# The border between mixer and up projection in a set order per engine, with the second pair's raw weights and a second h tile in finished rows

## The chip, the cores and the metric

The kernel runs on one core of a Trainium2 chip. The metric is the device time of one execution in microseconds (us); the figure of a kernel is the median of three runs. TensorE is called PE here, its weight loads PEld, VectorE DVE, ScalarE ACT, GpSimd POOL, and SyncE, which issues all the DMAs, SP.

## The reference

One layer of a streaming encoder for 1024 prompt frames and 64 sample frames, model width 1024. It has a mixer (two kinds of attention and a gating block, then one output projection) and an MLP with squared ReLU, each followed by a residual sum and a layer norm. What counts here is the seam between the two:

```python
x = layer_norm(ALPHA * x + mix, ln1_g, ln1_b)            # (1024 + 64, 1024)
h = jnp.square(jax.nn.relu(x @ w_up))                    # w_up   (1024, 4096)
x = layer_norm(ALPHA * x + h @ w_down, ln2_g, ln2_b)     # w_down (4096, 1024)
```

## The kernel before

Matrices are multiplied in three fp32r passes (high x high, high x low, low x high): every operand is split into a rounded copy, which ACT writes, and the rest, which DVE or POOL subtracts (`split`, `lo_sub`, L97).

**The mixer's tail.** Frames stand in nine tiles of 128 rows (the ninth has the 64 sample rows), taken in the order 0, 1, 4, 5, 8, 2, 6, 3, 7. `mix(t)` multiplies a tile with w_out (L232), adds the residual (L237) and norms it (`layer_norm`, L125 to L139): moments on DVE, the inverse root on POOL, scaling on ACT, the gain on POOL, the bias on DVE. The result, x1, stays in a tile `y` (tag `row`, seven buffers) and is stored to DRAM (L249).

**The up projection** is a Strassen-like scheme. Per pair p of weight blocks (256 of the 4096 columns, two f halves of 128) seven products stand in for eight. Seven combinations of the frames (`xo`) are made once by `x_pair`: transposes of y tiles on PE (L1127), sums (L1142 to L1151), splits. The frames are in two sets: s=0 (288 columns: tiles 0, 1, 4, 5 and the samples) and s=1 (256: tiles 2, 3, 6, 7). Seven combinations of W_up are made per pair by `prep`: three are splits of the raw weights (`wa`, L1182, the rest on POOL), four come from `w_sums` (L1190 to L1193, DVE, in place over the raw weights) and are split after that (`ws`, L1457 and L97).

A `Chain(p, s)` does the seven products of pair p and set s, twelve matmuls each (L1242). PSUM banks: A three times in turn, B, C, and D twice. ACT copies the A banks (L1253); DVE adds the banks into h (L1256 to L1262). The seventh product opens bank D again, so it must wait until L1256 has read D. Then come `relu` (L1274) and `sums` (L1283 to L1286) and the stores of h to DRAM (L1287, L1288, L1291).

**The border** is pair 0 and the start of pair 1. Pair 0's raw weights are loaded early; chain (0, 0) and then chain (0, 1) keep h in one set of buffers, `h7` (tag `wq`, one buffer) and `h1`. All mixer tiles lie in a pool `sp`. Only when it is closed (`p12.close()`) is the pool `lp` opened, over the same addresses, and pair 1's raw weights `wr1` are loaded into it. Pairs 1 to 12 run both chains product by product.

**What sets the order.** A scheduler places each engine's instructions by its own estimates, except inside `in_order(...)`, which chains every instruction of an engine to the one recorded before it. In the kernel before that is used only at the later border, from the up to the down projection.

Of the kernel before, what the change touches and what calls it, by code (L numbers as in the profile page):

```python
# [56 lines left out]
def _build(nc, tc, a, es):  # L57
# [151 lines left out]
    def mix(t, sa):  # L209
# [7 lines left out]
        y = ys[t] = two_halves(f"y{t}", None, None)  # L217
# [3 lines left out]
        for half in range(2):  # L221
# [46 lines left out]
    with ExitStack() as p1:  # L268
        sa = p1.enter_context(tc.tile_pool(name="sa", bufs=1, side="right"))

# [481 lines left out]
        def sgu_v(wv):  # L752
            wst = sp.tile([P, 4, 2, P], F32R, name="wst", tag="cc0")
# [5 lines left out]
            bs = sp.tile([P, 4], F32, name="bs")  # L759
# [351 lines left out]
    xs = p12.enter_context(tc.tile_pool(name="xs", bufs=1, side="right", reuse_waits="tile"))  # L1111
# [7 lines left out]
    def x_steps(nm, s, c0, n, r0, n0, r1, n1):  # L1119
# [31 lines left out]
        nc.vector.tensor_tensor(tt[:, 3], tt[:, 1], p21, op=ALU.subtract)  # L1151
        if s == 0:
# [160 lines left out]
    x23 = [x_pair(2), x_pair(3)]  # L1313
# [4 lines left out]
    def x_next(n):  # L1318
        for _ in range(n):
            while x23:  # L1320
                if next(x23[0], StopIteration) is StopIteration:
                    x23.pop(0)
                    continue
                break

    def first_chain(s, weave):
# [5 lines left out]
        h7 = sp.tile([P, 7, NS[s]], F32, name=f"h7_{s}", tag="wq", bufs=1)  # L1332
        h1 = sp.tile([P, 1, NS[s]], F32, name=f"h1_{s}", tag="raw", bufs=2)

        def hh(a, b):

            if a == 4:
                return h1
            return h7[:, a:b] if b <= 4 else h7[:, a - 1:b - 1]

        ch = Chain(0, s, Some(), hh, ((2, 4), (4, 5), (5, 6)))
        for i in range(7):
            ch.product(i)
            if weave:
                x_next(2)

    x_next(3)
    first_chain(0, True)
    x_next(99)
    first_chain(1, False)  # L1350
    p12.close()


    lp = es.enter_context(tc.tile_pool(name="lp", bufs=1, side="left", reuse_waits="tile"))
# [84 lines left out]
    with ExitStack() as p3:  # L1439
        rp = p3.enter_context(rp)  # L1440

        def prep(p, rest=True):
            raw = lp.tile([P, KT, 256], F32, name=f"wr{p}", tag="wr")
            nc.sync.dma_start(raw, w_up[:, :, p * 256:(p + 1) * 256])
# [3 lines left out]
            f0, f1 = raw[:, :, 0:P], raw[:, :, P:256]  # L1448
            a, b = slice(0, 4), slice(4, 8)
            for o, src in ((0, f0[:, a]), (1, f0[:, b]), (2, f1[:, b])):  # L1450
                split(wa[:, o, 0], wa[:, o, 1], src, nc.gpsimd)
            def summed():
                w_sums(f0, f1)

            def high():
                for q in (a, b):
                    nc.scalar.activation(ws[:, 0, q], raw[:, q], AF.Copy)  # L1457

            def low():
                lo_sub(nc.vector, ws[:, 1], raw, ws[:, 0])  # L1460
# [14 lines left out]
        prep(1)  # L1475
        for p in range(1, NP - 3):
# [524 lines left out]
```

## Time and profile before

| what | value |
|---|---|
| median of 3 runs | 1420.37 us (1419.03 to 1420.98) |
| profiled execution | 1420.73 us, span 1419.0 us |
| PE busy in the span | 1327.6 us (94%), 8827 matmuls |
| DVE / ACT / POOL busy | 1000.0 (70%) / 720.6 (51%) / 612.2 (43%) us |
| chain that ended last, by engine | PE 62%, DVE 11%, DMA 8%, POOL 7% |

The span runs from the first to the last instruction; what is left of the execution's time, 1.7 us, lies around it. In the timeline views a row is a run of like instructions in time: start, time from the start of its first to the end of its last, engine, line and tiles, count, and in square brackets the idle time of the engine just before it with what ended it.

### The profile page before, as it was taken

The numbers are of one execution on the slowest core, as the hardware profiler recorded it, in microseconds if no ns is written. First come the engines' busy times: TensorE is split into PE (matmuls) and PEld (weight loads), VectorE is DVE, ScalarE is ACT, GpSimd is POOL, SyncE is SP. The second block draws the span as 40 slices with busy tenths as digits, with TensorE's granted clock in tenths as the row PEclk, the third lists the DMA queues.
The fourth block names the chain that finished last, engine by engine and source line by source line (L and its number), as shares of the span: only waits on it lengthen the run. The fifth ranks groups of instructions, "written<-read, shape, count | busy, mean of one in ns | idle before, by whom it ended". The sixth has DMA issues, their size and how long they took to land.

```text
span 1419.0 us, 24283 instructions
## 1 busy us (share of the span) xinstructions
PE 1327.6 (94%) x8827; PEld 1210.9 (85%) x8827; DVE 1000.0 (70%) x1797; ACT 720.6 (51%) x1561; POOL 612.2 (43%) x665
## 2 busy tenths in 40 slices
PE   7999999999989997998969999999989999999996
PEld 6899999999888996876859999999977778887875
DVE  3567566676786599877836787687668677677676
ACT  3366555666664475333413332322237677667765
POOL 2222222266564446655412222122146765555647
PEclk9999999999999998999989999999999999999999
DMA  7324232322313424432033443443378343344343
GB/s 216 77 78 112 61 109 66 81 66 55 79 27 83 130 86 135 130 108 78 32 112 116 166 138 116 165 138 124 134 233 300 118 165 136 122 160 140 109 134 127
DMA packets 148177, 168.86 MB, mean 119 GB/s; under 512 B 27085, under 2 KB 114445, under 8 KB 148057
## 3 DMA queue, kind: packets, MB, share of 16 engines
q1 hardware_dynamic: 148056, 167.30, 37.8%
q8 instruction: 70, 1.15, 0.3%
q14 instruction: 51, 0.41, 0.1%
HBM read 109.26 MB, written 51.71 MB: 113 GB/s over the span
## 4 chain that ended last, share of the span: by engine, by line
PE 62%; DVE 11%; DMA 8%; POOL 7%; issue 5%; ACT 5%; SPq 1%; DVEq 0%; ACTq 0%; POOLq 0%
PE zA L1242 9%; PE zD L1242 6%; PE mx L232 6%; PE kvsb L337 5%; PE kvfox L337 4%; PE A L1630 4%; PE zB L1242 3%; PE zC L1242 3%; DMA rd<-w_down 2%; POOL rd L1387 2%; POOL wd L97 2%; PE qfox L478 2%; PE qsb L478 2%; PE Sfox L536 2%; PE D L1630 2%
## 5 line engine op out<-in xcount | busy, mean ns | idle before, releaser
L97 POOL TENSOR_TENSOR wa<-wr,wa 128x512 fp32r<-128x512 f32 x45 | 67.9, 1536 | 232.0 <-ACT wa L1182 232.0
L97 POOL TENSOR_TENSOR wd<-rd,wd 128x512 fp32r<-128x512 f32 x77 | 101.5, 1328 | 123.4 <-ACT wd L1182 113.5
L232 PE MATMUL mx<-xT,oTb 128*128 128x512 f32 (+1 forms) x416 | 107.0, 409 | 3.3 <-ACT oTb L191 2.3
L1242 PE MATMUL zD<-xo,ws 128*128 128x288 f32 (+1 forms) x720 | 99.1, 292 | 8.6 <-DVE hh L1256 8.6
L1242 PEld LDWEIGHTS zD<-xo,ws 128*128 128x128 f32 x720 | 94.9, 191 | 9.3 <-DVE hh L1256 9.3
L232 PEld LDWEIGHTS mx<-xT,oTb 128*128 128x128 f32 (+1 forms) x416 | 77.5, 191 | 23.1 <-ACT oTb L191 3.3
L1242 PE MATMUL zA<-xo,ws 128*128 128x288 f32 (+1 forms) x720 | 97.1, 289 | 0.0
L337 PE MATMUL kvfox<-wkvfox,xT 128*128 128x256 f32 (+3 forms) x624 | 91.3, 296 | 3.0 <-DVE fx L440 1.9
L1242 PEld LDWEIGHTS zA<-xo,ws 128*128 128x128 f32 x720 | 93.5, 189 | 0.0
L522 POOL TENSOR_TENSOR sgsb<-sgsb,snsb 128x127 f32<-128x127 f32 (+7 forms) x48 | 58.8, 1227 | 78.4 <-DVE snsb L520 63.9
L1182 ACT ACTIVATE wd<-rd 128x512 fp32r<-128x512 f32 x105 | 63.9, 624 | 55.3 <-POOL rd L1387 26.4
L337 PE MATMUL kvsb<-wkvsb,xT 128*128 128x256 f32 (+1 forms) x624 | 87.7, 286 | 0.0
L1387 POOL TENSOR_TENSOR rd<-rd 128x512 f32<-128x512 f32 x56 | 79.7, 1423 | 17.7 <-DVE b L97 15.4
L337 PEld LDWEIGHTS kvfox<-wkvfox,xT 128*128 128x128 f32 (+1 forms) x624 | 82.5, 196 | 4.6 <-DVE fx L440 2.2
L1630 PE MATMUL A<-wd,wd 128*128 128x512 f32 x312 | 82.5, 396 | 3.0 <-DVE acc L1597 2.8
L520 DVE TENSOR_TENSOR_SCAN snsb<-snsb,one 128x128 f32<-128x128 f32 (+7 forms) x48 | 72.1, 1506 | 13.2 <-ACT snsb L519 12.7
L1253 ACT ACTIVATE sn<-zA 128x256 f32<-128x256 f32 (+1 forms) x80 | 31.1, 390 | 95.8 <-PE zA L1242 86.4
L337 PEld LDWEIGHTS kvsb<-wkvsb,xT 128*128 128x128 f32 (+1 forms) x624 | 79.2, 187 | 0.2
L1630 PEld LDWEIGHTS A<-wd,wd 128*128 128x128 f32 x312 | 58.2, 188 | 18.6 <-DVE acc L1597 4.1
L1630 PE MATMUL A<-wd,h4a 128*128 128x512 f32 x240 | 64.6, 394 | 0.0
L1242 PE MATMUL zA<-xo,wa 128*128 128x288 f32 (+1 forms) x360 | 50.2, 293 | 10.2 <-ACT wa L1182 10.2
L1457 ACT ACTIVATE ws<-wr 128x1024 fp32r<-128x1024 f32 x30 | 31.1, 1057 | 56.0 <-DVE wr L1192 56.0
(524 smaller groups left out, 3748.7 us busy)
## 6 DMA issues: line engine op xcount, KB each, us to landing
wr<-w_up SPq DMA_DIRECT2D x15, 1024.0 KB, 5.5
h_dr<-hh SPq DMA_DIRECT2D x30, 512.0 KB, 3.2
rd<-w_down SPq DMA_DIRECT2D x30, 512.0 KB, 4.3
awa<-h_dr SPq DMA_DIRECT2D x30, 512.0 KB, 4.0
hr<-h_dr SPq DMA_DIRECT2D x32, 384.0 KB, 4.7
h_dr<-hh SPq DMA_DIRECT2D x30, 384.0 KB, 4.2
raw<-w_in SPq DMA_DIRECT2D x44, 256.0 KB, 3.4
xr<-x_prompt SPq DMA_DIRECT2D x8, 512.0 KB, 6.5
```

Source lines behind the costliest of these rows:

```text
L97: eng.tensor_tensor(out, src, hi.bitcast(F32), op=ALU.subtract)
L232: nc.tensor.matmul(acc[0:m], oT[:, k, hx, 0:m], wo[k // 4][hw][:, k % 4, cs], start=(i == 0), stop=(i == len(seq) - 1))
L337: nc.tensor.matmul(acc[0:n, c0:c0 + n1 - n0], xT[k // 4][:, k % 4, c:c + n], wt[:, k, hw, n0:n1], start=(i == 0), stop=(i == len(seq) - 1))
L478: nc.tensor.matmul(acc[:, 0:w], wq[:, k, hw, :], xT[k // 4][:, k % 4, c:c + w], start=(i == 0), stop=(i == len(seq) - 1))
L520: nc.vector.tensor_tensor_scan(g[:, 0:n][:, ::-1], g[:, 0:n][:, ::-1], one.broadcast_to([P, n]), 1.0, op0=ALU.mult, op1=ALU.bypass)
L522: nc.gpsimd.tensor_tensor(s[:, 0:n - 1], s[:, 0:n - 1], g[:, 1:n], op=ALU.mult)
L1182: nc.scalar.activation(hi, raw, AF.Copy)
L1242: nc.tensor.matmul(z, w[:, hw, k], xop(s, bo, hx)[:, k, :], start=(new and k == 0 and j == 0), stop=(k == 3 and j == 2), skip_group_check= ...
L1253: nc.scalar.activation(c, z, AF.Copy)
L1387: eng.tensor_tensor(r[:, o], r[:, x], r[:, y], op=ALU.subtract)
L1457: nc.scalar.activation(ws[:, 0, q], raw[:, q], AF.Copy)
L1630: nc.tensor.matmul(z, h[:, hx, q, o], wset[self.c % 2][q][:, hw, wb], start=((n in (0, 3) or n == 1 and self.c == 0) and q == 0 and j == 0 ...
```

## The change

It does the following.

- `layer_norm` becomes a generator `norm_steps` in three steps (moments, scale and gain, bias); for the last mixer tile, 7, the steps are taken one by one in the border.
- The border, from tile 7's norm to pair 1's first chain, is recorded inside `in_order(border)`.
- Pair 1's raw W_up is loaded as two f halves of 512 KB into the rows of x1 of tiles 2 and 6 (`raws1`), whose values have been stored and transposed. `prep` takes such a pair of halves; its splits and sums then work on two tiles of 128x8x128, not on one of 128x8x256.
- Chain (0, 1) keeps h in the rows of tiles 3 and 7 (`h44`), not in the tile of chain (0, 0).
- `lp` is opened ahead of chain (1, 0), which is recorded whole inside the set order; then come `prep(2)` and chain (1, 1), which the scheduler places. Pairs from 2 on are recorded as before.
- Three small tiles (`sel2`, `wst`, `bs`) move from pool `sp` to `sa`, and the pool `xs` of the transposes gets an exit of its own.

```diff
-            nc.vector.tensor_tensor(h, h, bb[0:n, c], op=ALU.add)
+            if not acts:
+                nc.vector.tensor_tensor(h, h, bb[0:n, c], op=ALU.add)
+        yield
...
+        h44 = [yrow[t].rearrange("p (b c) -> p b c", b=4) for t in (3, 7)]
+        return Chain(0, s, Some(), lambda a, b: h44[a // 4][:, a % 4:(b - 1) % 4 + 1], ((2, 4), (4, 6)))
...
-    x_next(3)
-    first_chain(0, True)
-    x_next(99)
-    first_chain(1, False)
-    p12.close()
...
+    with in_order(border):
+        ln = norm_steps(sp, ys[t], P, env["g1"], env["b1"], f"a{t}", True)
+        next(ln)
+        next(x2)
+        c0 = first_chain(0)
+        c0.product(0)
...
+        raws1 = [yrow[t].rearrange("p (k c) -> p k c", k=KT) for t in (2, 6)]
+        for f in range(2):
+            nc.sync.dma_start(raws1[f], w_up[:, :, 256 + f * P:256 + (f + 1) * P])
+        x1_store(t)
...
+        c1 = first_chain(1)
+        c1.product(0)
+        for _ in x3:
+            pass
+        c1.product(1)
+        c0.relu()
+        c1.product(2)
+        c0.sums()
+    xss.close()
...
+        with in_order(border):
+            summed, high, low = prep(1, False, raws1)
+            c1.product(3)
+            summed()
+            c1.product(4)
+            high()
+            c1.product(5)
+            low()
+            c1.product(6)
+        p12.close()
+
+        lp = es.enter_context(tc.tile_pool(name="lp", bufs=1, side="left", reuse_waits="tile"))
+        with in_order(border):
+            ch = chain(1, 0)
+            for i in range(7):
+                ch.product(i)
+        prep(2)
```

The built programs differ in the border alone: on PE the 2054 rows of the program ahead of it and the 827 rows from pair 4's second product on are the same. In the rows below, names have lost the first number: `zA_0_` is bank A of set 0, `zA_1_` of set 1; `y_8335`, `y_8482`, `y_8592` and `y_8676` are the rows of x1 of tiles 2, 6, 3 and 7. The lines of the changed kernel are 20 higher in the Chain (L1256 becomes L1276, L1274 becomes L1294, L1283 to L1286 become L1303 to L1306), L1190 to L1193 become L1210 to L1213.

PE, the end of pair 0 and the start of pair 1, before:

```order
L1242 MATMUL zC_1_9035<-xo_8760,w_3_8716 128x256 x2
L1242 MATMUL zA_1_8967<-xo_8760,oTb 128x256 x12
L1242 MATMUL zC_1_9035<-xo_8760,w_3_8716 128x256 x10
L1242 MATMUL zD_1_9008<-xo_8759,oTb 128x256 x12
L1242 MATMUL zA_0_9117<-xo_7973,wa_9081 128x288
L1242 MATMUL zA_1_9131<-xo_8759,wa_9081 128x256
L1242 MATMUL zB_0_9145<-xo_7973,wa_9081 128x288
L1242 MATMUL zB_1_9159<-xo_8759,wa_9081 128x256
```

and in the changed kernel:

```order
L1262 MATMUL zD_1_9020<-xo_8744,oTb 128x256 x12
L1262 MATMUL zA_1_8947<-xo_8745,oTb 128x256 x12
L1262 MATMUL zC_1_9053<-xo_8745,w_3_8716 128x256 x12
L1262 MATMUL zD_1_9020<-xo_8744,oTb 128x256 x12
L1262 MATMUL zA_0_9096<-xo_7973,wa_9012 128x288 x12
L1262 MATMUL zB_0_9110<-xo_7973,wa_9012 128x288 x12
L1262 MATMUL zA_1_9218<-xo_8744,wa_9012 128x256 x12
L1262 MATMUL zB_1_9232<-xo_8744,wa_9012 128x256 x12
```

Products are whole there; the last one of pair 0 (bank D for the second time) still stands just ahead of pair 1.

DVE, the end of chain (0, 0) and the start of chain (0, 1), before:

```order
L1274 SCALAR_TENSOR_TENSOR h_0_8796<-h_0_8796 128x576
L1283 TENSOR_TENSOR h_0_8796<-h_0_8797,h_0_8796 128x256
L1286 TENSOR_TENSOR h_0_8796<-h_0_8796,h_0_8797 128x256
L1284 TENSOR_TENSOR h_0_8796<-h_0_8796 128x256
L1285 TENSOR_TENSOR h_0_8796<-h_0_8796 128x256
L1258 TENSOR_TENSOR h_1_8965<-zB_1_8981,sn_1_0_8962 128x256
L1256 TENSOR_TENSOR h_1_8965<-zD_1_9008,sn_1_2_8964 128x256
```

and in the changed kernel:

```order
L1278 TENSOR_TENSOR y_8592<-zB_1_8969,sn_1_0_8944 128x256
L1294 SCALAR_TENSOR_TENSOR h_0_8829<-h_0_8829 128x576
L1294 SCALAR_TENSOR_TENSOR h_0_8830<-h_0_8830 128x288
L1294 SCALAR_TENSOR_TENSOR h_0_8829<-h_0_8829 128x288
L1303 TENSOR_TENSOR h_0_8829<-h_0_8830,h_0_8829 128x256
L1304 TENSOR_TENSOR h_0_8829<-h_0_8829 128x256
L1305 TENSOR_TENSOR h_0_8829<-h_0_8829 128x256
L1306 TENSOR_TENSOR h_0_8829<-h_0_8829,h_0_8830 128x256
L1210 TENSOR_TENSOR y_8482<-y_8482 128x512
L1211 TENSOR_TENSOR y_8482<-y_8335,y_8482 128x512
L1212 TENSOR_TENSOR y_8335<-y_8482,y_8335 128x512
L1213 TENSOR_TENSOR y_8335<-y_8335 128x512
L1276 TENSOR_TENSOR y_8676<-zD_1_9020,sn_1_2_8946 128x256
```

The first add of chain (0, 1) has moved ahead of chain (0, 0)'s end, and the four sums of pair 1's weights stand ahead of the add that frees bank D.

SP, the stores and loads of the border, before:

```order
L249 DMA x_dr<-y_8592 128x512 x2
L249 DMA x_dr<-y_8676 128x512 x2
L1291 DMA hs_dr<-h_0_8796 128x32
L1291 DMA hs_dr<-h_0_8797 128x32
L1291 DMA hs_dr<-h_0_8796 128x2x32
L1287 DMA h_dr<-h_0_8796 512x1x256
L1288 DMA h_dr<-h_0_8796 384x1x256
L1287 DMA h_dr<-h_1_8965 128x1024
L1288 DMA h_dr<-h_1_8965 128x768
L1444 DMA wr_9079<-w_up 128x8x256
L1444 DMA wr_9096<-w_up 128x8x256
```

and in the changed kernel:

```order
L267 DMA x_dr<-y_8592 128x512 x2
L1381 DMA y_8335<-w_up 128x8x128
L1381 DMA y_8482<-w_up 128x8x128
L267 DMA x_dr<-y_8676 128x512 x2
L1307 DMA h_dr<-h_0_8829 512x1x256
L1308 DMA h_dr<-h_0_8829 384x1x256
L1311 DMA hs_dr<-h_0_8829 128x2x32
L1311 DMA hs_dr<-h_0_8830 128x32
L1311 DMA hs_dr<-h_0_8829 128x32
L1307 DMA h_dr<-y_8592 128x1024
L1308 DMA h_dr<-y_8676 128x768
L1491 DMA wr_9199<-w_up 128x8x256
```

Pair 1's weights have moved from behind both chains' stores to ahead of tile 7's store; pair 2's load is now the first behind them.

## Rows read from the trace of the kernel before

**Rows 1.** Busy time per stretch: bounds, length, PE, PEld, DVE, ACT, POOL; PEclk, DMA, GB/s.

```profile
700.00:720.00 20.00, 15.45 (x116) 14.96 (x116) 14.22 (x25) 5.48 (x11) 4.07 (x3) 0.91 0.19 63
720.00:730.00 10.00, 0.04 (x1) 0.04 (x1) 2.12 (x6) 0.72 (x2) 0.00 (x0) 0.65 0.59 197
730.00:740.00 10.00, 10.00 (x67) 9.96 (x68) 5.12 (x6) 3.76 (x6) 3.75 (x3) 0.83 0.01 2
...
800.00:1000.00 200.00, 200.00 (x1589) 200.00 (x1588) 151.90 (x220) 55.72 (x105) 48.00 (x30) 1.00 0.42 141
```

**Rows 2.** Timeline of PE through the border, from the mixer's last products to pair 2.

```profile
676.01 11.37 PE L232 MATMUL mx<-xT,oTb 128*128 128x512 f32 x48
687.22 0.60 PE L1127 MATMUL xta<-ident,y 128*128 128x128 f32 x4
687.65 0.60 PE L1127 MATMUL xtd<-ident,y 128*128 128x128 f32 x4
...
696.51 1.86 PE L1242 MATMUL zA<-xo,oTb 128*128 128x288 f32 x12 [1.72 <-ACT sn L1253]
...
700.44 0.66 PE L1127 MATMUL xtd<-ident,y 128*128 128x128 f32 x4 [0.88 <-DVE h L1256]
...
702.52 1.57 PE L1242 MATMUL zA<-xo,w 128*128 128x256 f32 x12
...
716.78 2.93 PE L1242 MATMUL zD<-xo,oTb 128*128 128x256 f32 x12 [3.83 <-DVE h L1256]
729.96 0.82 PE L1242 MATMUL zA<-xo,wa 128*128 128x288 f32 x2 [10.24 <-ACT wa L1182]
...
731.62 3.68 PE L1242 MATMUL zA<-xo,wa 128*128 128x288 f32 x22
...
741.19 2.96 PE L1242 MATMUL zA<-xo,ws 128*128 128x288 f32 x22
...
759.17 1.77 PE L1242 MATMUL zC<-xo,wa 128*128 128x288 f32 x12
760.78 3.07 PE L1242 MATMUL zA<-xo,ws 128*128 128x288 f32 x23
```

**Rows 3.** Timeline of DVE in the same stretch.

```profile
695.85 1.75 DVE L139 TENSOR_TENSOR y<-y,gb 128x512 f32<-128x512 f32 x1 [2.29 <-POOL y L138]
...
704.40 1.28 DVE L97 TENSOR_TENSOR xo<-tt,xo 128x512 fp32r<-128x512 f32 x2
...
708.73 0.76 DVE L1274 SCALAR_TENSOR_TENSOR h<-h 128x576 f32<-128x576 f32 x1
709.41 1.52 DVE L1283 TENSOR_TENSOR h<-h,h 128x256 f32<-128x256 f32 x1
...
715.98 0.42 DVE L1258 TENSOR_TENSOR h<-zB,sn 128x256 f32<-128x256 f32 x1 [3.92 <-DMA h_dr<-h]
...
733.83 0.69 DVE L1190 TENSOR_TENSOR wr<-wr 128x512 f32<-128x512 f32 x1 [11.60 <-POOL wa L97]
...
736.00 0.69 DVE L1193 TENSOR_TENSOR wr<-wr 128x512 f32<-128x512 f32 x1
```

**Rows 4.** Timeline of POOL in the same stretch.

```profile
709.08 1.57 POOL L97 TENSOR_TENSOR xo<-tt,xo 128x512 fp32r<-128x512 f32 x1 [2.26 <-ACT xo L1160]
730.04 3.75 POOL L97 TENSOR_TENSOR wa<-wr,wa 128x512 fp32r<-128x512 f32 x3 [19.39 <-ACT wa L1182]
```

**Rows 5.** Timeline of ACT in the same stretch.

```profile
704.41 0.63 ACT L1160 ACTIVATE xo<-tt 128x512 fp32r<-128x512 f32 x1
...
709.20 0.38 ACT L1253 ACTIVATE sn<-zA 128x256 f32<-128x256 f32 x1 [0.20 <-PE zA L1242]
```

**Rows 6.** The chain that ended last, in order of time: start, length, what.

```profile
712.34 3.51 DMA h_dr<-h
...
722.70 6.50 DMA wr<-w_up
```

**Rows 7.** Pair 0's raw weight loads (tile ru, two of 512 KB): issue to landing.

```profile
DMA to landing us min/median/max: 5.5/5.5/5.5
```

More of the change, by code (lines that the diff above doesn't have):

```diff
@@ L138, in layer_norm @@
             nc.gpsimd.tensor_tensor(h, h, gb[0:n, c], op=ALU.mult)
-            nc.vector.tensor_tensor(h, h, bb[0:n, c], op=ALU.add)
+            if not acts:
+                nc.vector.tensor_tensor(h, h, bb[0:n, c], op=ALU.add)
+        yield
+        if acts:
+            for i in range(2):
+                h = y[i][0:n]
+                nc.vector.tensor_tensor(h, h, bb[0:n, i * 512:(i + 1) * 512], op=ALU.add)
     def mix_open():
@@ L216, in mix @@
         preps(at + 2, sa)
-        y = ys[t] = two_halves(f"y{t}", None, None)
+        r = yrow[t] = sp.tile([P, D], F32, name=f"y{t}", tag="row", bufs=ROWS)
+        y = ys[t] = [r[:, 0:512], r[:, 512:D]]
         for i in range(2):
@@ L1110, in _build @@
     xo1 = []
-    xs = p12.enter_context(tc.tile_pool(name="xs", bufs=1, side="right", reuse_waits="tile"))
+    xss = ExitStack()
+    xs = xss.enter_context(tc.tile_pool(name="xs", bufs=1, side="right", reuse_waits="tile"))
     def xop(s, o, h):
@@ L1151, in x_steps @@
         nc.vector.tensor_tensor(tt[:, 3], tt[:, 1], p21, op=ALU.subtract)
+        yield
         if s == 0:
@@ L1316, in _build, with first_chain @@
             pass
[L1318 to L1326, printed above, removed]
+    def first_chain(s):
         sn = [sp.tile([P, 288], F32, name=f"sn0_{s}_{q}", tag="gl", bufs=3) for q in range(2 + s)]
@@ L1331, in __getitem__ @@
                 return sn[at[1]][:, at[2]]
[L1332 to L1345, printed above, removed]
@@ L1347, in _build, with hh @@
-    x_next(3)
-    first_chain(0, True)
-    x_next(99)
-    first_chain(1, False)
-    p12.close()
-    lp = es.enter_context(tc.tile_pool(name="lp", bufs=1, side="left", reuse_waits="tile"))
+        if s == 0:
+            h = []
+            def hh(a, b):
+                if not h:
+                    h.append(sp.tile([P, 7, NS[s]], F32, name=f"h7_{s}", tag="wq", bufs=1))
+                    h.append(sp.tile([P, 1, NS[s]], F32, name=f"h1_{s}", tag="raw", bufs=2))
+                if a == 4:
+                    return h[1]
+                return h[0][:, a:b] if b <= 4 else h[0][:, a - 1:b - 1]
+            return Chain(0, s, Some(), hh, ((2, 4), (4, 5), (5, 6)))
@@ new lines, in first_chain @@
+        h44 = [yrow[t].rearrange("p (b c) -> p b c", b=4) for t in (3, 7)]
+        return Chain(0, s, Some(), lambda a, b: h44[a // 4][:, a % 4:(b - 1) % 4 + 1], ((2, 4), (4, 6)))
+    border = {}
+    t = ORD[-1]
+    next(x2)
+    with in_order(border):
+        ln = norm_steps(sp, ys[t], P, env["g1"], env["b1"], f"a{t}", True)
+        next(ln)
+        next(x2)
+        c0 = first_chain(0)
+        c0.product(0)
+        next(x2)
+        next(ln)
+        next(x2)
+        for _ in ln:
+            pass
+        c0.product(1)
+        c0.product(2)
+        for _ in x2:
+            pass
+        raws1 = [yrow[t].rearrange("p (k c) -> p k c", k=KT) for t in (2, 6)]
+        for f in range(2):
+            nc.sync.dma_start(raws1[f], w_up[:, :, 256 + f * P:256 + (f + 1) * P])
+        x1_store(t)
+        c0.product(3)
+        next(x3)
+        c0.product(4)
+        next(x3)
+        next(x3)
+        c0.product(5)
+        next(x3)
+        c0.product(6, False)
+        c1 = first_chain(1)
+        c1.product(0)
+        for _ in x3:
+            pass
+        c1.product(1)
+        c0.relu()
+        c1.product(2)
+        c0.sums()
@@ L1451, in prep @@
                 split(wa[:, o, 0], wa[:, o, 1], src, nc.gpsimd)
+            whole = len(raw) == 3
+            parts = ((slice(0, 256), raw[2]),) if whole else ((slice(0, P), f0), (slice(P, 256), f1))
             def summed():
@@ L1455, in high @@
             def high():
-                for q in (a, b):
-                    nc.scalar.activation(ws[:, 0, q], raw[:, q], AF.Copy)
+                for q in (a, b) if whole else (slice(0, 8),):
+                    for c, src in parts:
+                        nc.scalar.activation(ws[:, 0, q, c], src[:, q], AF.Copy)
             def low():
-                lo_sub(nc.vector, ws[:, 1], raw, ws[:, 0])
+                for c, src in parts:
+                    lo_sub(nc.vector, ws[:, 1, :, c], src, ws[:, 0, :, c])
             if rest:
@@ L1473, in chain @@
             return Chain(p, s, sn, lambda a, b: h8[:, a:b], ((2, 6),))
-        prep(1)
-        for p in range(1, NP - 3):
+        with in_order(border):
[14 more added lines that the diff above has]
+        prep(2)
+        ch = chain(1, 1)
+        for i in range(7):
+            ch.product(i)
+        for p in range(2, NP - 3):
             prep(p + 1)
```

36 lines of the change are left out of this document (22 added, 14 removed).

## The prediction

> **What bounds the kernel now.** I read the busy time per stretch first. From 800 to 1000 us PE is busy for all of 200 us at the full clock, so whatever the border saves is neither given back nor hidden there: the pairs behind it just start earlier [rows 1]. From 700 to 730 us, in the border, PE is busy for 15.5 us of 30, and the clock falls to 0.65 of full in the last ten [rows 1]. The PE timeline tells where: waits of 1.72, 0.88, 3.83 and 10.24 us, 16.7 us in all [rows 2]. The last two are one cause in two places, storage for pair 0's second h and for pair 1's raw weights. At 715.98 DVE waits 3.92 us for a store of h, since chain (0, 1) writes the buffers that chain (0, 0) is still storing [rows 3]; the store took 3.51 us [rows 6]. PE's second D product waits behind that. Then the load of pair 1's weights, which needs the whole pool closed, starts at 722.70 and takes 6.50 us, with PE empty until ACT and POOL have split the first block [rows 2, 6].
>
> The clock adds to it. The twelve D matmuls at 716.78 took 2.93 us, where twelve of the same shape took 1.57 earlier: 1.4 us lost. After the long wait 22 matmuls took 3.68 us, against 2.96 later, and the six before them took 1.66 us (729.96 to 731.62) where 2.96 x 6/22 = 0.81 is normal: 0.7 + 0.9 = 1.6 us lost [rows 2]. So the border costs 16.7 + 1.4 + 1.6 = **19.7 us** now. That is the most there is to win.
>
> **What the change takes away.** Chain (0, 1) writes into rows 3 and 7, which no store of h holds: the 3.92 us wait of DVE goes. Its cover is that x1 of tiles 3 and 7 is stored by then; those stores stand on SP ahead of all stores of h. Pair 1's weights are issued once the last transpose of tile 2 has read the rows, at about 691 us (the mixer's products end at 687.2 and some 4 us of work stand before that transpose). Two like loads took 5.5 us each [rows 7], so they land at about 697, or 698 at the 6.50 us of the larger one [rows 6]; ACT reaches their first split after 709. The load is hidden with more than 10 us to spare, and the 10.24 us wait goes. Tile 7's store stands behind these loads on SP, but nothing reads it before the down projection. Moving three small tiles and the exit of `xs` changes no order ahead of the border: nothing. The splits of two half tiles in place of one whole tile move as many elements: nothing.
>
> **What comes in its place.** PE first. Its products end at 687.22, and some 0.3 us earlier here, since two matmuls of 288 columns that stood ahead of them (twelve take 1.77 us at 759.17) now stand behind: 686.9. Up to the second D product of chain (0, 1) it has seven groups of transposes at 0.43 us (687.22 to 687.65), seven products of 288 columns at 1.61 (759.17 to 760.78) and six of 256 columns at 1.61 x 256/288 = 1.43 [rows 2]: 3.0 + 11.3 + 8.6 = 22.9 us, so 709.8 without a wait. On the way there are small ones. Transposes and bank C share two PSUM buffers, and in the set order they come closer together: the third transpose group waits for DVE to read the first (1.0 us), C of chain (0, 0) waits for DVE, which itself waits for ACT's copy of the third A (1.7 us), and three splits come 0.2 us late each. I take 3.2 us, an estimate from laying the instructions of the four engines end to end with their durations in rows 2 to 5; the bounds are 0 and twice the 2.6 us of such waits now (1.72 and 0.88). PE is then at the second D product at 713.0.
>
> That product needs DVE's add L1276, the first read of bank D. On DVE the chain (0, 0)'s three relu and four sums stand before it, then the four weight sums, and the first of these overwrites what POOL's last `wa` split reads. I lay that out from the last split of tile pair 3. PE has made chain (0, 1)'s first product at 686.9 + 3.0 + 11.3 + 3.2 + 1.4 = 705.8. ACT copies it (0.38), then splits the transposed sums (0.63 for the first), and DVE subtracts two of them (1.28): 708.1 [rows 3, 5]. From here POOL has five subtractions, two for the frames and three for pair 1's weights, at 1.25 each (3.75 for three): 6.3 us [rows 4]. DVE has three relu of 0.76 and twice about 0.4, and four sums of about 0.4, 2.8 us without their overlaps.
>
> These two do not run side by side. At 709.41 a DVE sum of 256 columns took 1.52 us rather than 0.4 and ended just after POOL's subtraction at 709.08, which itself took 1.57 us rather than 1.25; the add at 695.85 took 1.75 us [rows 3, 4]. So with both operands in SBUF the one waits for the other, and the lengths add: 708.1 + 6.3 + 2.8 = 717.2. The four weight sums follow at 0.72 each (733.83 to 736.00 is three of them): 2.9 us, then L1276 with 0.42: 720.5 [rows 3]. **PE waits 720.5 - 713.0 = 7.5 us.** The Trainium skill says the same of this pair in "SBUF — State Buffer", section "Who interferes with whom": a DVE instruction with two SBUF inputs and a GpSimd one that reads SBUF shut each other out for a whole instruction. By that rule the wait is the 7.5 us; without it POOL would end at 714.4, DVE's seven would be done by then, and the wait would be 4.8 us. The rows above bear the rule out.
>
> After a wait of this kind PE starts at the low clock. The price is that after the long wait now, 1.6 us [rows 2]. What follows does not hold PE up. `ws` of pair 1 is ready some 3 us after L1276, and four `wa` products of about 6 us stand before the first use of it. DVE then waits, in order, for the store of chain (0, 1)'s h out of tile 7's row before it may write pair 1's h, which lies there: issued at about 727 and 3.51 us long [rows 6], so until 731. Behind it on DVE stand all adds of pair 1; PE needs the first of them at the seventh product of pair 1, some 16 us after 722. Pair 2's load is issued at about 727, lands at 733 or 734, and PE needs it 20 us after 722, at 742.
>
> **The sum.** 19.7 - (3.2 + 7.5 + 1.6) = 7.4 us saved. The profiled execution took 1420.73 us, so 1413.3; the median of the three runs lies 0.4 lower, and from there it is **1413.0 us**.
>
> **Rivals.** (1) *The exclusion of DVE and POOL costs little*, because they happen to fall beside each other: then the wait on bank D is 4.8 us, and 2.7 more are saved: 1410.3. For it: not every pair of the kind in the trace is stretched, as the two subtractions at 704.40 took 0.64 each [rows 3]. Against it: at 709.41 the very instructions collided. With the small waits at 0 as well it is 1407.1.
>
> (2) *The clock stays low for longer.* PE's clock was 0.65 and 0.83 in the two stretches after 720 [rows 1]. If after 720.5 it stays at half, 1.2 GHz, for 10 us of work rather than about 3, it loses 5 us, not 1.6: 1416.4. Against it: now it was back at full (2.4 GHz) some 3 us after work resumed, after a longer wait.
>
> (3) *The change doesn't do what it says*: the two loads are issued late, since SP takes its queue in order and stands behind the stores of tile 3, and POOL's third split then waits for weights. From a landing later than about 714, 16 us after the estimate, each us costs PE a us; with 6 us of that nearly all of the gain is eaten: about 1419. The rows speak against it: by 695.85 only tile 7's norm is left, so tile 3's stores are out before [rows 3].
>
> (4) *Slower: the store that pair 1's h waits for.* This is the wait that the change removes (3.92 us at 715.98), put back at a later place. It decides from the point where the store out of tile 7's row lands after 737, 10 us after its issue; beyond that PE is held at pair 1's seventh product for each us, and past 18 us the whole 7.4 us are gone; at 22 us it is 1424. Against it: the like store took 3.51 us, and the largest load 6.50 [rows 6].
>
> **Chances.** Forecast 0.62 (1411 to 1415), rival 1 0.12, rival 2 0.14, rival 3 0.08, rival 4 0.04. A measurement of this kernel can tell about 0.2%, 2.8 us, from no change. Rivals 1 and 2 and the forecast are faster by more than that: 0.88; rival 3 is within it: 0.08; rival 4 slower: 0.04. The range takes in rival 1 and rival 2 and leaves out rivals 3 and 4 and the far ends: 1409.0 to 1416.6.
>
> **What the new profile would show.** PE's wait of 10.24 us ahead of pair 1 and DVE's wait for a store ahead of chain (0, 1) are gone; in their place one wait of 7 to 8 us ahead of twelve D matmuls of 256 columns, released by DVE's add of bank D, with the weight sums L1210 to L1213 just before it on DVE, and relu and sums stretched to over 1 us beside POOL. The two weight loads land before 700. From pair 2 on PE has no wait. Wrong would be a wait of PE for a split of the weights, a wait between pairs 1 and 2, or one on bank D under 4 or over 10 us.

## The result, and the profile of the changed kernel

| | before | after |
|---|---|---|
| median of the runs | 1420.39 us (4 runs, 1419.03 to 1420.98) | 1411.05 us (4 runs, 1408.07 to 1412.26) |
| span of the profiled execution | 1419.0 us | 1409.4 us |
| mean granted TensorE clock | 0.976 | 0.977 |

The ratio of the times is 0.9932 with an interval of 0.9915 to 0.9950: the changed kernel is faster by 9.3 us by the medians, and by 7 to 12 us within the interval. The forecast was 1413.0 us, a gain of 7.4.

Where the gain lies is read from two products of bank B, both the first of pair 4, behind which the programs are the same. The first fence is the PE timeline of before (start, length, engine, line, operation, tiles, shape, count, idle time before and its releaser). The rows of these two products end where the view was cut off, so only their starts count.

```profile
798.29 0.97 PE L1242 MATMUL zB<-xo,wa 128*128 128x288 f32 x6
```

The second is the PE timeline of the changed kernel.

```profile
674.80 11.45 PE L244 MATMUL mx<-xT,oTb 128*128 128x512 f32 x48
...
689.72 0.63 PE L1146 MATMUL xtc<-ident,y 128*128 128x128 f32 x4 [1.00 <-DVE tt L1161]
...
699.69 1.83 PE L1262 MATMUL zC<-xo,w 128*128 128x288 f32 x12 [1.66 <-DVE tt L1161]
...
709.52 1.58 PE L1262 MATMUL zA<-xo,oTb 128*128 128x256 f32 x12
710.94 1.58 PE L1262 MATMUL zC<-xo,w 128*128 128x256 f32 x12
718.87 2.93 PE L1262 MATMUL zD<-xo,oTb 128*128 128x256 f32 x12 [6.36 <-DVE y L1276]
721.59 2.15 PE L1262 MATMUL zA<-xo,wa 128*128 128x288 f32 x12
723.58 1.75 PE L1262 MATMUL zB<-xo,wa 128*128 128x288 f32 x12
...
788.61 1.63 PE L1262 MATMUL zB<-xo,wa 128*128 128x288 f32 x11
```

Pair 4 starts 798.29 - 788.61 = 9.7 us earlier, which is the whole difference of the spans (9.6). The mixer's last 48 products started 1.2 us earlier, at 674.80 and not 676.01 [rows 2]; of that 0.3 are the two matmuls that moved behind them, the other 0.9 lie ahead of the border, where the programs are the same. So the border saves 8.8 us. The waits say nearly the same: of [rows 2], 3.83 and 10.24 us are gone, and the waits are 1.00, 1.66 and 6.36, 9.0 us in all. Twelve D matmuls at half clock took 2.72 us to the next start where twelve took 1.42 at 709.52, and the twelve behind them 1.99 where 1.61 is normal: 1.7 us. That leaves 10.7 of 19.7 us, a gain of 9.0.

Busy time per stretch, after (length; PE, PEld, DVE, ACT, POOL; granted clock, DMA share, GB/s):

```profile
700.00:720.00 20.00, 13.51 (x105) 12.93 (x104) 16.64 (x24) 6.81 (x13) 7.47 (x5) 0.89 0.16 50
720.00:730.00 10.00, 10.00 (x74) 10.00 (x74) 5.95 (x11) 1.38 (x3) 0.00 (x0) 0.88 0.48 160
720.00:722.00 2.00, 2.00 (x11) 2.00 (x11) 2.00 (x3) 0.58 (x1) 0.00 (x0) 0.50 0.00 0
```

Against [rows 1], PE is busy for all of the ten microseconds from 720 now, the first of them at half clock (granted clock 0.50, that is 1.2 of 2.4 GHz), and DVE and POOL are busier from 700 to 720. The timeline of DVE shows with what:

```profile
707.29 0.42 DVE L1278 TENSOR_TENSOR y<-zB,sn 128x256 f32<-128x256 f32 x1
707.62 4.47 DVE L1294 SCALAR_TENSOR_TENSOR h<-h 128x576 f32<-128x576 f32 x3
712.13 1.38 DVE L1303 TENSOR_TENSOR h<-h,h 128x256 f32<-128x256 f32 x1
...
714.94 0.42 DVE L1305 TENSOR_TENSOR h<-h 128x256 f32<-128x256 f32 x1
...
715.62 0.68 DVE L1210 TENSOR_TENSOR y<-y 128x512 f32<-128x512 f32 x1
...
718.40 0.42 DVE L1276 TENSOR_TENSOR y<-zD,sn 128x256 f32<-128x256 f32 x1
...
728.68 0.79 DVE L1278 TENSOR_TENSOR hh<-zB,sn 128x288 f32<-128x288 f32 x2 [3.41 <-DMA h_dr<-y]
```

and that of POOL beside it:

```profile
707.16 3.14 POOL L97 TENSOR_TENSOR xo<-tt,xo 128x512 fp32r<-128x512 f32 x2 [8.61 <-ACT xo L1180]
710.25 4.38 POOL L97 TENSOR_TENSOR wa<-y,wa 128x512 fp32r<-128x512 f32 x3
```

DVE has no wait from 707.29 to L1276, and PE's product waits for that one add of 0.42 us. The relu and the first two sums are stretched as long as POOL is at work, to 714.63 (710.25 + 4.38); the two sums behind that take 0.42 again. SP's timeline, the profile's DMA issues (count, KB each, us from issue to landing) and ACT's timeline put the loads in place:

```profile
690.38 1.01 SPq L1381 DMA_DIRECT2D y<-w_up  x2
```

```profile
y<-w_up SPq DMA_DIRECT2D x2, 512.0 KB, 5.0
```

```profile
708.65 1.66 ACT L1202 ACTIVATE wa<-y 128x512 fp32r<-128x512 f32 x3
...
732.04 1.67 ACT L1202 ACTIVATE wa<-wr 128x512 fp32r<-128x512 f32 x3 [0.39 <-DMA wr<-w_up]
```

Pair 1's loads are issued at 690.4, take 5.0 us and wait 13 us for ACT; pair 2's splits wait 0.39 us for theirs, and PE for none.

### The profile page after: what moved, and what is told of

It is laid out like the page before. It is cut to its first block, busy times and chain, and to the rows that moved or that the text cites. A ratio compares the mean times of both kernels' runs of the same rounds, so it can differ in the third digit from the quotient of the medians.

```text
span 1409.4 us, 24290 instructions
## 1 busy us (share of the span) xinstructions
PE 1328.3 (94%) x8827; PEld 1212.0 (86%) x8827; DVE 1006.1 (71%) x1797; ACT 721.0 (51%) x1561; POOL 615.4 (44%) x665
## 4 chain that ended last, share of the span: by engine, by line
PE 69%; DVE 11%; DMA 5%; issue 5%; POOL 5%; ACT 4%; SPq 1%; DVEq 0%; ACTq 0%; POOLq 0%
PE zA L1262 9%; PE A L1702 8%; PE zD L1262 6%; PE mx L244 6%; PE kvsb L355 5%; PE kvfox L355 4%; PE D L1702 4%; PE zB L1262 3%; PE zC L1262 3%; PE B L1702 2%; PE qfox L496 2%; PE Sfox L554 2%; DVE snsb L538 2%; PE qsb L496 1%; PE ptfox L602 1%
## 5 line engine op out<-in xcount | busy, mean ns | idle before, releaser
L97 POOL TENSOR_TENSOR wa<-wr,wa 128x512 fp32r<-128x512 f32 x42 | 64.9, 1573 | 221.4 <-ACT wa L1202 221.4
L1262 PE MATMUL zD<-xo,ws 128*128 128x256 f32 (+1 forms) x720 | 99.6, 293 | 8.7 <-DVE hh L1276 8.7
L1702 PEld LDWEIGHTS A<-wd,h4a 128*128 128x128 f32 x240 | 45.5, 190 | 11.1 <-DVE h4a L1463 0.7
```

Of the source, the lines that this page charges most:

```text
L97: eng.tensor_tensor(out, src, hi.bitcast(F32), op=ALU.subtract)
L1262: nc.tensor.matmul(z, w[:, hw, k], xop(s, bo, hx)[:, k, :], start=(new and k == 0 and j == 0), stop=(k == 3 and j == 2), skip_group_check= ...
L1702: nc.tensor.matmul(z, h[:, hx, q, o], wset[self.c % 2][q][:, hw, wb], start=((n in (0, 3) or n == 1 and self.c == 0) and q == 0 and j == 0 ...
```

## The experiments

Each edit is made to the changed kernel, unless another is named. Executions of one kernel spread by 2 to 10 us, and much of that lies outside the border: the mixer's last products start at 670.9 to 676.0 us in these profiles, behind equal instructions, and from pair 4 to the end pass 617.9 to 623.6 us. So a time is given with its ratio to the kernel before that ran beside it (median 1417.4 to 1418.7 us), and verdicts rest on the waits and on the length of the border. That is taken from each PE timeline as the time from the last transposes ahead of the mixer's last 48 products (675.31 in the kernel before, 674.45 in the changed one) to pair 4's first product of bank B:

| kernel | border, us |
|---|---|
| before | 123.0 |
| the changed kernel, first and second profile (e4) | 114.2, 115.1 |
| e1, e2 | 113.0, 113.3 |
| e3, e11 | 123.7, 123.4 |
| e5, e6 | 116.2, 116.3 |
| e7, e8 | 109.6, 111.6 |
| e9, e10 | 104.8, 104.8 |
| e12 | 119.2 |

### e4_after_again

No edit.

> No edit: the changed kernel once more, beside the others. 1411.0 us (1408 to 1412.5); the wait ahead of the D products 6.4 us within 0.5. If the wait is the same and the time differs by 1 us or more, the difference lies in the stages ahead of the border.

1411.73 us, ratio 0.9948 (0.9928 to 0.9967). PE's timeline:

```profile
714.89 2.93 PE L1262 MATMUL zD<-xo,oTb 128*128 128x256 f32 x12 [6.53 <-DVE y L1276]
717.62 3.08 PE L1262 MATMUL zA<-xo,wa 128*128 128x288 f32 x12
720.50 1.84 PE L1262 MATMUL zB<-xo,wa 128*128 128x288 f32 x12
```

The wait is the same within 0.2 us. The low clock lasted longer: from 714.89 to 720.50 are 5.6 us where 3.0 is normal (1.42 + 1.61), a loss of 2.6 us, not 1.7. So the price of one such spell differs by 0.9 us from one execution to the next of the same program, and the border is 0.9 us longer. The profiled execution, 1405.16 us, was 6.0 us shorter than the first one all the same: 3.9 us lie ahead of the border and 2.9 behind pair 4, so not only ahead, as I expected. Against the kernel before the change gains 7.4 us by this ratio and 7.9 on the border.

### e1_wsums_late

```diff
             c1.product(3)
-            summed()
             c1.product(4)
+            summed()
             high()
```

> Edit: the four sums of pair 1's raw weights (L1210 to L1213) stand on DVE behind the add of bank D (L1276) instead of ahead of it; nothing else is moved by hand. Both theories expect PE's wait ahead of the twelve D products to fall from 6.4 us by the length of the four sums, 2.8 us, to 3.6 us. Theory A (what is won at one wait is kept): the time falls by 2.8 us and a little of the clock, 1411.0 to about 1408. Theory B (a second wall stands close behind): pair 2's load can be issued only after chain (0, 1)'s h is stored, DVE's work up to that store is no shorter, and the load lands at about 732 as now; PE, which is 2.8 us earlier, stands about 3 us before pair 1's second D product or pair 2, so the time stays at 1410 to 1412. My stake is on B, 0.6 to 0.4.

1410.07 us, ratio 0.9938 (0.9919 to 0.9957).

```profile
715.91 2.93 PE L1262 MATMUL zD<-xo,oTb 128*128 128x256 f32 x12 [3.76 <-DVE y L1276]
...
737.74 1.87 PE L1262 MATMUL zD<-xo,ws 128*128 128x288 f32 x12 [0.27 <-DVE hh L1276]
```

The wait falls by 2.6 us, about the length of the four sums. My stake, a second wall of 3 us, is wrong: the wall costs 0.27 us. The clock fell all the same, and until 721.52 it cost 2.6 us as in the second execution above, so about 1.4 us of the 2.6 stay against the first profile (1.1 on the border), less than theory A has. The time alone, 1 to 1.7 us better, tells nothing against the spread.

### e2_wa_on_dve

```diff
-                split(wa[:, o, 0], wa[:, o, 1], src, nc.gpsimd)
+                split(wa[:, o, 0], wa[:, o, 1], src, nc.vector if p == 1 else nc.gpsimd)
```

> Edit: the three subtractions of pair 1's wa go from POOL to DVE, in the same place of the order. Theory A (DVE and POOL shut each other out): the third relu and the four sums of chain (0, 0) fall back from 1.4 or 1.5 us to 0.4 to 0.8 us each, the three subtractions take 0.65 us each on DVE, and although DVE has 2 us more to do, its add of bank D ends 0.5 to 1.5 us earlier: PE's wait falls from 6.4 to 5 to 6 us and the time to 1409.5 to 1410.5. Rival (the relu and sums are long for a reason of their own, such as their waits on each other): they stay at 1.4 us, DVE gets the three subtractions on top, the wait grows by about 2 us to 8.3, the time to 1413.

1408.88 us, ratio 0.9931 (0.9914 to 0.9949). DVE's timeline, then PE's:

```profile
706.14 3.36 DVE L1294 SCALAR_TENSOR_TENSOR h<-h 128x576 f32<-128x576 f32 x3
709.53 0.43 DVE L1303 TENSOR_TENSOR h<-h,h 128x256 f32<-128x256 f32 x1
...
711.13 1.89 DVE L97 TENSOR_TENSOR wa<-y,wa 128x512 fp32r<-128x512 f32 x3
```

```profile
716.32 2.93 PE L1262 MATMUL zD<-xo,oTb 128*128 128x256 f32 x12 [5.47 <-DVE y L1276]
```

DVE does three subtractions more and is done 0.9 us earlier. The sums take 0.43 us, the three relu 3.36 rather than 4.47: only POOL's two subtractions for the frames still stand beside them. Theory A holds in the wait and in the lengths; the time lies 0.6 us below its range, which the spread covers. The rival, which had the wait at 8.3 us, falls.

### e3_raw_in_pool

```diff
-        raws1 = [yrow[t].rearrange("p (k c) -> p k c", k=KT) for t in (2, 6)]
-        for f in range(2):
-            nc.sync.dma_start(raws1[f], w_up[:, :, 256 + f * P:256 + (f + 1) * P])
...
-            summed, high, low = prep(1, False, raws1)
...
+            for i in range(3, 7):
+                c1.product(i)
...
         with in_order(border):
+            prep(1)
             ch = chain(1, 0)
```

> Edit: one part undone. Pair 1's raw weights are loaded as one tile of 1 MB into the pool that opens once the old one is closed, as before the change; chain (0, 1)'s h stays in rows of x1, and the set order stays. My theory: the load can be issued only when chain (0, 0)'s h is stored, at about 717, lands at about 723 to 725, PE waits about 12 to 14 us ahead of pair 1 and 2 to 4 us more in it for the splits; the wait ahead of the D products falls to 1 to 2 us, since neither the weight sums nor POOL's three subtractions are there. Together about 10 us lost: 1421 (1419 to 1424), all of the gain. Rival (the set order and the rows for h carry a good part of the gain): 1415 to 1417.

1419.97 us, ratio 1.0011 (0.9998 to 1.0024), and a border of 123.7 us: the whole gain is gone.

```profile
710.19 1.65 PE L1262 MATMUL zD<-xo,oTb 128*128 128x256 f32 x12 [0.75 <-DVE y L1276]
724.55 0.82 PE L1262 MATMUL zA<-xo,wa 128*128 128x288 f32 x2 [12.71 <-ACT wa L1202]
```

The wait ahead of the D products shrinks to 0.75 us (1 to 2 were expected), as weight sums and POOL's three subtractions are no longer there, and the long wait for the load is back, 12.71 us. The set order and the rows for h, which are still there, earn nothing together.

### e5_c0_early and e6_c0_early_h_in_sp

Chain (0, 0)'s relu and sums at once behind its last add; in the second kernel, besides, chain (0, 1)'s h back in the buffers of chain (0, 0).

```diff
-        c0.product(6, False)
+        c0.product(6)
...
-        c0.relu()
         c1.product(2)
-        c0.sums()
```

> Edit: chain (0, 0)'s relu and sums stand on DVE right behind its last add (L1282), ahead of the low parts of tile pair 3, instead of behind them; h of chain (0, 1) stays in the rows of x1. Theory: the seven instructions then run before POOL starts its five subtractions and are not stretched; they take about 3.3 us rather than 8.0. The low parts come 3 us later, so PE waits about 2.8 us ahead of chain (0, 1)'s third product; the wait ahead of the twelve D products falls from 6.4 to 1 to 3.5 us, set by POOL's last wa subtraction and the four weight sums. Net 1 to 2 us won: 1409 to 1410. Rival (the DVE work, wherever it stands, sets the end): waits of 2.8 and 6 us, 1413 to 1414.

> Edit: as the run before it, and one part undone: chain (0, 1)'s h lies again in the two buffers that hold chain (0, 0)'s h, so that DVE's first add of chain (0, 1) waits for the stores of chain (0, 0). Theory: with the sums this early the stores are issued at about 707.5 and land at 711 to 712, so the add comes about 3 us later than in the run before it, but the weight sums behind it wait for POOL until about 713.5 anyway: same time within 1 us as that run, and the rows of x1 for h are worth nothing by themselves once the order is set so. Rival (the rows for h carry their share, the 3.9 us wait of before): 3 to 4 us slower than the run before it.

1411.83 us (0.9955, 0.9941 to 0.9969) and 1411.29 us (0.9955, 0.9940 to 0.9969). DVE's timeline of the first, and PE's of the first:

```profile
702.75 1.49 DVE L1294 SCALAR_TENSOR_TENSOR h<-h 128x576 f32<-128x576 f32 x3
...
705.87 3.44 DVE L97 TENSOR_TENSOR xo<-tt,xo 128x512 fp32r<-128x512 f32 x2
```

```profile
707.67 2.50 PE L1262 MATMUL zA<-xo,oTb 128*128 128x256 f32 x10 [2.59 <-DVE xo L97]
...
718.32 2.93 PE L1262 MATMUL zD<-xo,oTb 128*128 128x256 f32 x12 [3.83 <-DVE y L1276]
```

The three relu take 1.49 us with POOL idle, as expected, and the first wait is 2.59 us. But no time is won (the border is 1 to 2 us longer than the changed kernel's), and the expectation of 1409 to 1410 misses in three places: DVE's two low parts now stand beside POOL's and take 3.44 us (1.28 in [rows 3]), the wait ahead of D is 3.83 us, above the range that I gave, and the clock falls behind each of the two waits. The stretching was moved, not removed. The second kernel equals the first within 0.5 us, and within 0.1 on the border: there the rows for h are worth nothing, as the theory had it, and its rival (3 to 4 us) falls.

### e7_d_first and e8_d_first_relu_late

```diff
-        c0.relu()
         c1.product(2)
-        c0.sums()
...
             c1.product(3)
-            summed()
             c1.product(4)
+            c0.relu()
+            summed()
             high()
+            c0.sums()
             c1.product(5)
```

with pair 1's `wa` on DVE as in e2_wa_on_dve. In e8, `c0.relu()` stands behind `high()`, and the end is `c1.product(6, False)`, `c0.sums()`, `c1.finish()`.

> Edit: three moves at once that the runs so far point to. On DVE the add of bank D (L1276) stands directly behind chain (0, 1)'s first add and the three wa subtractions, which go to DVE; behind it stand chain (0, 0)'s relu, the four weight sums, chain (0, 0)'s sums. Theory: PE's wait ahead of the D products is gone (under 0.5 us), and with it the half clock behind it; PE then meets smaller waits, about 1 us for the bank at pair 1's first D product of the second chain and 1 to 3 us at pair 2's weights, whose load is issued only when chain (0, 1)'s h is stored. Net 4 us: 1407 (1405 to 1408.5), border shorter by 3.5 to 5 us. Rival (the wall behind is solid: pair 2's load lands no earlier and PE stands for it as long as it was early): border as the changed kernel's within 1.5 us, 1410 to 1411.

> Edit: as the run before it, with chain (0, 0)'s relu and sums still later: relu behind the weight sums, sums behind the low part of ws and the last add of chain (0, 1). Theory: no wait at pair 1's first D product of the second chain, but the stores of chain (0, 1)'s h come about 1.7 us later and so does pair 2's load; PE waits about 2 us ahead of pair 2. Same as the run before it within 1 us. Rival (the wall is the load of pair 2 alone): 1.7 us slower than the run before it.

1406.49 us (0.9911, 0.9888 to 0.9935) and 1408.06 us (0.9927, 0.9906 to 0.9948). PE's timeline of e7 (the second D products), a stretch of it, and PE's timeline and a stretch of e8:

```profile
710.11 1.53 PE L1262 MATMUL zD<-xo,oTb 128*128 128x256 f32 x12
```

```profile
720.00:730.00 10.00, 9.56 (x75) 9.35 (x74) 2.18 (x6) 2.26 (x5) 1.14 (x1) 1.00 0.58 197
```

```profile
733.37 0.61 PE L1262 MATMUL zA<-xo,wa 128*128 128x288 f32 x1 [2.70 <-ACT hh L1273]
```

```profile
730.00:740.00 10.00, 7.30 (x35) 6.89 (x34) 4.53 (x8) 4.00 (x7) 3.74 (x3) 0.66 0.06 19
```

In e7 the wait ahead of the D products is gone and the clock stays full; behind it small waits of 0.3 to 1.0 us remain, 2.5 us in all, and 4.6 us are won against the first measurement (4.6 on the border too), as expected. In e8 the waits behind the D products are one of 2.70 us, with half clock behind it. It is 1.6 us slower than e7, 2.0 on the border; the intervals of the times overlap, so the border decides. That is near the rival's number (1.7), but not for the rival's reason alone: pair 2's load is issued only 0.6 us later than in e7, counted from the mixer's last products (49.8 and 49.2 us), and the waits sum to nearly the same. What e8 loses is mostly the half clock: 24 matmuls from 733.86 took 5.6 us where 3.0 is normal.

### e9_no_set_order, e10_no_set_order_h_in_sp, e12_no_set_order_raw_in_pool

The border's three `in_order` blocks become blocks without effect, so that the scheduler places the border again; storage and code stay.

```diff
-    with in_order(border):
+    with ExitStack():
         ln = norm_steps(sp, ys[t], P, env["g1"], env["b1"], f"a{t}", True)
```

e10 has besides the code of e6, with h of chain (0, 1) in the old buffers; e12 the load of e3.

> Edit: one part undone. Storage stays as in the changed kernel (pair 1's weights and chain (0, 1)'s h in rows of x1, the norm in steps, the code in the same sequence), but the border's order per engine isn't set: it is left to the scheduler, as before the change. It spreads the work otherwise: chain (0, 0)'s relu and sums stand one by one between the steps of tile pair 3 and are over by about 711, and the four weight sums come behind the add of bank D. Theory (the gain comes from storage, and the set order costs time by what it lines up ahead of the add of bank D): PE has waits of 0.4 to 1.2 us, about 3 us in all, no half clock; the border is 7 to 9 us shorter than the changed kernel's and the time 1403 (1402 to 1405). Rival (the set order carries part of the gain, and without it waits come back elsewhere): 1411 or more.

> Edit: as the run before it, and chain (0, 1)'s h in the buffers of chain (0, 0) again. Theory (the rows for h are worth nothing once chain (0, 0)'s sums are early): its add waits for a store that lands at about 712 to 714, PE does not wait for it; same as the run before it within 1 us. Rival (the 3.9 us wait of before returns and PE waits for it): 3 to 4 us slower than the run before it.

> Edit: as the run without a set order, and pair 1's weights loaded as one tile of 1 MB into the new pool again; chain (0, 1)'s h stays in rows of x1. It closes the square of two parts, set order and rows for the weights. Theory (the rows for the weights are the whole gain, and the rows for h and the code's new sequence are worth nothing without them): one long wait ahead of pair 1, 12 to 14 us, released by ACT's split, half clock behind it; 1417 to 1419, the time of the kernel before, within 1.5 us. Rival (the rows for h, which remove DVE's wait of 3.9 us, carry 3 to 4 us by themselves): 1414.

1400.63 us (0.9879, 0.9860 to 0.9897), 1400.77 us (0.9873, 0.9852 to 0.9893) and 1415.15 us (0.9975, 0.9964 to 0.9985). PE's timeline of e9 and a stretch of it, then DVE's of e9:

```profile
672.04 0.60 PE L1146 MATMUL xtb<-ident,y 128*128 128x128 f32 x4
...
692.10 1.86 PE L1262 MATMUL zA<-xo,oTb 128*128 128x288 f32 x12 [0.55 <-ACT sn L1273]
...
696.00 0.66 PE L1146 MATMUL xtd<-ident,y 128*128 128x128 f32 x4 [0.88 <-DVE h L1276]
...
709.53 2.91 PE L1262 MATMUL zA<-xo,wa 128*128 128x256 f32 x22
712.27 1.53 PE L1262 MATMUL zD<-xo,oTb 128*128 128x256 f32 x12
...
777.01 3.04 PE L1262 MATMUL zB<-xo,wa 128*128 128x288 f32 x23
```

```profile
700.00:720.00 20.00, 19.84 (x163) 19.56 (x162) 15.99 (x28) 6.98 (x13) 7.43 (x5) 1.00 0.17 56
```

```profile
708.06 0.42 DVE L1276 TENSOR_TENSOR y<-zD,sn 128x256 f32<-128x256 f32 x1 [1.21 <-ACT sn L1273]
...
711.90 0.69 DVE L1210 TENSOR_TENSOR y<-y 128x512 f32<-128x512 f32 x1 [1.19 <-POOL wa L97]
```

By the medians the kernel without the set order is 10.4 us faster than with it, 16.8 us faster than before, and the fastest of all. The medians with and without were not taken side by side; the border bears the difference out: 104.8 us (777.01 - 672.04, less 0.13 for one matmul of the row that runs earlier), 9.3 to 10.2 less than in the two profiles with the order. 1400.63 us lies below the 1402 to 1405 expected. PE waits 1.6 us in all (0.55, 0.88 and 0.16). Three things differ on the rows: chain (0, 0)'s relu and sums are spread and largely over before POOL's subtractions; the add of bank D comes at 708.06, ahead of the weight sums at 711.90 that wait for POOL; and PE has matmuls of pair 1 ahead of the second D products, so that it would have work if the add were late. What each of the three is worth is not shown apart; e7, which puts the add first by hand and pair 1's subtractions on DVE, gets 4.6 us of the 10. e10 is equal within 0.2 us: with the weights in rows, the rows for h are worth nothing here either.

e12 refutes the expectation beside it: 1415.15 us, not 1417 to 1419, and the rival's 1414 is nearer. PE's timeline, the chain that ended last (start, length, what), and that of the kernel before:

```profile
722.36 0.82 PE L1262 MATMUL zA<-xo,wa 128*128 128x288 f32 x2 [12.32 <-ACT wa L1202]
```

```profile
712.85 3.06 DMA h_dr<-y
...
716.04 5.55 DMA wr<-w_up
```

```profile
722.25 0.34 SPq L1288
```

Measured from the mixer's last products (672.29 here, 676.01 in [rows 2]), the last store of h is issued at 40.6 us and not at 46.2, since DVE's 3.92 us wait is gone and its sums come sooner. But here the load stands behind the landing of that store (712.85 + 3.06), where before it followed the store's issue at 722.25 by 0.45 us; so it is issued at 43.8 and not at 46.7 [rows 6], only 2.9 us earlier. It also took 5.55 us, not 6.50; why is not shown. In e3 the load stands behind the landing of the store in the same way (715.25 + 2.71, load at 718.10). So the rows for h and the code's new sequence, which were not taken apart, are worth 3.6 us together (3.8 on the border) as long as the load has to wait for those stores; once it doesn't, the rows for h are worth nothing (e10).

### e11_load_late

```diff
         c1.product(2)
         c0.sums()
+        for f in range(2):
+            nc.sync.dma_start(raws1[f], w_up[:, :, 256 + f * P:256 + (f + 1) * P])
```

> Edit: in the changed kernel, the two loads of pair 1's weights are issued behind the stores of chain (0, 0)'s h, at about 716 instead of 690, and land at about 722. Theory (a late load holds more than its own split, since PE's second D product waits for DVE's L1276, which stands behind the weight sums, which wait for POOL's last wa subtraction): L1276 comes at about 729, PE waits some 15 us there in place of 6.4, the time is 1420 to 1422, and the loads now have about 13 us to spare before they cost anything. Rival (they cost only what they land behind PE's first use of wa): 2 to 3 us, 1414.

1417.61 us, ratio 1.0005 (0.9986 to 1.0024). The chain that ended last (first fence) and PE's timeline:

```profile
713.02 3.97 DMA y<-w_up
```

```profile
724.78 2.93 PE L1262 MATMUL zD<-xo,oTb 128*128 128x256 f32 x12 [14.94 <-DVE y L1276]
```

The wait is the 15 us expected, the time 2.4 us under the range. From landing (717.0) to the D products pass 7.8 us: ACT's splits, POOL's, the weight sums, L1276. In the changed kernel the D products come at 718.87, so a landing up to 711 would have cost nothing there; with the loads down at 695.4 they have some 15 us to spare.

## Why the prediction was right

**What the change takes away** came as worked out. DVE's wait of 3.92 us is gone (L1278 at 707.29 follows without one), and PE's of 10.24 us. The loads were issued at 690.4 and down at 695.4; said were 691 and 697. e3_raw_in_pool shows that without the weights' rows nothing of the gain is left; the rows for h, which the prediction also credited with one of the two waits, are worth nothing in two other orders with the weights in rows (e6, e10), and up to 3.6 us, together with the code's new sequence, where the weights' rows are missing (e12). In this kernel's own order they can't be taken out alone, since chain (0, 1)'s first add L1278 stands ahead of chain (0, 0)'s relu and would overwrite its h. The prediction didn't ask what either part is worth alone.

**What comes in its place** was the right wait at the right place: PE ahead of the second D products, released by L1276, with the weight sums just ahead of it. Its size, 7.5 us, was too large; it was 6.36 and 6.53. The term most at fault is the adding of lengths, 708.1 + 6.3 + 2.8. From the start of POOL's subtractions to the end of the sums that is 9.1 us; measured are 715.62 - 707.16 = 8.5. That is 0.6 of the 1.1 us. Another 0.3 is PE, which came to the product 26.4 us after the mixer's end (686.09) and not 26.1; there two errors nearly cancel by luck, since the small waits were 0.5 us shorter and the work 0.9 longer (23.8 us, not 22.9). The mechanism itself is shown by e2 and e5: three relu take 1.49 us with POOL idle, 3.36 beside two of its subtractions, 4.47 beside more. But POOL pays little: five subtractions took 7.5 us where five times 1.25 is 6.3. So a DVE instruction of this kind is held up for some 1.0 us, most of one subtraction, while POOL loses 0.25 us for each of its own. DVE's adds out of a PSUM bank are not held up: L1278 at 707.29 took its 0.42 us beside POOL's subtraction at 707.16, and so did L1276 at 708.06 in e9, beside POOL's three from 707.63. The Trainium skill, "SBUF — State Buffer", section "Who interferes with whom", has a DVE instruction with two SBUF inputs and a GpSimd one that reads SBUF contend for a shared port that is an exclusive lock. Lengths that add up, the 9.1 us, are the estimate by it; the trace agrees in kind, and is 0.6 us below it in the sum.

**The small waits** were 1.00 and 1.66 us, said were 1.0 and 1.7; the three of 0.2 us don't show as waits, so 2.7 us are seen of 3.2. **The clock** cost 1.7 us, said was 1.6; the 2.6 us of the second execution say that so close a hit was in part luck.

**What follows holds nobody up**, as said: DVE waited for the store until 728.68 (said was 731), pair 2's load was down at 732.0 (733 or 734), and PE met no wait from pair 1 on.

**The sum**: 9.0 us by the listed waits and 8.8 by the start of pair 4, not 7.4. Of the 1.4 to 1.6 us that it was short by, 1.1 are the wait on bank D and the rest the small waits. The medians' 9.3 us can't be read to a tenth beside an interval of 7 to 12, and e4 has 7.4.

**The rivals.** (1), without the exclusion, had a wait of 4.8 us (4.7 by its own terms) and 1410.3 us. The measured 1411.05 lies nearer to that than to the forecast's 1413.0, so the time alone would not tell them apart; the 6.4 us of wait lie between the two, and e2 decides for the exclusion. The pair that the prediction counted for this rival, the two DVE subtractions at 704.40 [rows 3], does not speak for it: in the kernel before, POOL's subtraction beside them, at 705.12, took 1.71 us and not 1.25, and DVE's relu behind them, at 705.60, took 1.54 where another of its size took 0.70, so the two engines did collide there. (2), a longer half clock, didn't come: the product at 723.58 has its full speed again (1.75 us, as at 759.17 in [rows 2] 1.77); in e4 the half clock went on for 5.6 us, still short of the 10 us of work that this rival needs. (3) and (4) didn't either, and e11 puts a price on (3): a wait of 14.9 us and a ratio of 1.0005 for loads that land at 717.0, with a landing up to 711, not 714, that costs nothing. What the prediction did not name is the set order itself as a cost. It took the order for given and listed the waits in it; under the scheduler's order the same storage has 1.6 us of waits in place of 9.0 and no half clock (e9).

## What to carry to other kernels

Storage that lets a load start early was worth 14.5 us under the scheduler's order (e12 to e9; 14.4 on the border), and an order written by hand gave some 10 of it back; so time the new storage under the old order first, and test each part alone. In a hand-set order look at the one short instruction that frees a bank for the engine that sets the time, here an add of 0.42 us, and put everything that doesn't feed it behind it (e7). In this kernel bulk subtractions on POOL stretched DVE's relu, sums and subtractions with both operands in SBUF that fell beside them, so the sum of both engines' lengths, and not the longer one, came near the time (8.5 us for 9.1).

## What was not expected of the hardware

Two of DVE's 256-column sums took 1.38 us rather than 0.42 beside POOL, and three subtractions moved from POOL to DVE (1.89 us of DVE time) made DVE finish 0.9 us earlier, since POOL no longer held it. The half clock behind one and the same wait cost 1.7 us in one execution and 2.6 in the other. In these profiles the clock stayed full behind waits of 1.00 and 1.66 us and fell to half (granted clock 0.50) behind those of 2.59, 3.76 and 6.36, so that the two waits of e5 cost more than the one of the changed kernel although they sum to the same 6.4 us.
